# Four reorderings in a hybrid decoder step: early weight sums, gate read-outs, subtractions and state copies moved

## The chip, the cores and the metric

The kernel runs on one core of a Trainium2 chip. Its engines are TensorE (PE; its weight loads are listed apart as PEld), VectorE (DVE), ScalarE (ACT), GpSimd (POOL) and SyncE (SP), which here only issues DMAs. Time is measured on the device, from the start to the end of one execution, in microseconds.

## The reference, cut to what matters

One inference step of a two-layer decoder over 1048 tokens (16 meta tokens, 1024 of a prompt, 8 samples), in float32, model width 1024.

- Layer 0 projects the input, runs gated linear attention and a diagonal complex state-space model (S5) side by side, joins both and projects back (`w_out_0`).
- Layer 1 is a Griffin block: `y = (h * gelu(gate)) @ w_out`, where `h` is a gated linear recurrence over 1536 channels and `gate` a projection of the normalised input.
- Each layer ends in a gated feed-forward: `x + (gelu(conv(gate)) * val) @ w_down` with `gate, val = split(rmsnorm(x) @ w_up)` and `d_ff = 2816`.

```python
def rmsnorm(x, g):
    y = xf * lax.rsqrt(jnp.mean(xf * xf, axis=-1, keepdims=True) + EPS)
    return (y * g).astype(x.dtype)
...
xr, xi = xr + Ar * x0r - Ai * x0i, xi + Ar * x0i + Ai * x0r     # S5
...
y = (h * jax.nn.gelu(gate)) @ w_out                             # layer 1
...
return x + (jax.nn.gelu(gate) * val) @ w_down, new_buf          # feed-forward
```

## The kernel before

Every operand of a large matmul is split into a high part (cast to fp32r on ScalarE) and a low part (the rest, subtracted on VectorE), and each product is three matmuls (`mm3`): high by high, high by low, low by high. Lines 128, 129 and 130 are these three. Line 85 is the cast, line 45 the helper `tt` through which every elementwise operation of two tensors goes, on VectorE or, with the argument `P`, on GpSimd; line 48 is its form with a scalar. So rows are told apart by tile names. Line 147 is `colsum`, a product with a matrix of ones.

Weights come by `load_w`: a DMA on SP into `wraw`, a ring of three buffers, then the split into `whi` and `wlo`, rings of six. Products land in PSUM banks of two rings of four: `bank`, and `p` (tag `aux`). Each engine works through its own instructions in a fixed order, which the tile framework writes down before the run: it goes by the order in which the code is traced, by ready times that it estimates, and by priority (`tc.high_priority()`). A queue that waits holds back all that stands behind it on the same engine.

**S5.** The 32 groups go in four blocks (`b` = 0 to 3). `states(b)` forms the inputs in PSUM, moves them to `s5VR`, rotates them (`s5WC`, `s5WS`), scans them on VectorE into `s5ZB` and rotates them back: `ZA` and `VC` hold the products, and four subtractions or additions of 64 rows write the state, shifted by one, into `s5XP`. Line 466 multiplies `s5XP`, line 465 the input. `s5XR` and `s5SO` are the samples' step and the final states. `tables(b + 1)` builds `s5E`, which TensorE turns in line 366. Projections of the same layer lie between the blocks.

**First output projection.** Eight tiles `X`, three chunks each, are added to out of PSUM, stored to `xdn`, squared for the norm (`sq` on ScalarE, `acc` on GpSimd), and cut in halves for a seven-product scheme of block matrix multiplication (`Seven`): `B11`, `B21`, `B22` are plain halves, `T1` to `T4` sums of halves. `sums` forms these from tiles `t`.

**Layer 1.** Eight steps (two halves of the tokens by four groups of channels). A step projects (`xr`), applies the previous step's output projection (`out`), forms the gates, runs the recurrence (`rec`, scan in line 1540), and projects the gate branch: `gelu_branch` fills a bank per chunk of 262 tokens with 24 matmuls and reads it out into `rgg`. `joined` multiplies both. In the second half `before` begins the next feed-forward's statistics for finished tiles.

**The last step and the second feed-forward.** `out` ends the sums of `X`; `after` squares each chunk, and `sums_in` cuts it for `Seven`, in two parts; for the last two pairs the second part is kept in `rest` and traced after `out`. `ffn_up` makes 22 tiles `hidden(t)`, each of seven products: `B11`, `B21`, `T2`, `T3`, `T1`, `B22`, `T4`. Tiles 0 and 1 do their first two products ahead. The weights of four products are sums of blocks, formed by `sums` on GpSimd from tiles `wA` into `wS`. These pools lie where `X` was.

Of the kernel before, what the change touches and what calls it, by code (L numbers as in the profile page):

```python
# [9 lines left out]
F32 = mybir.dt.float32  # L10
# [29 lines left out]
def hybrid_step_kernel(ctx: ExitStack, tc: tile.TileContext, a: dict):  # L40
# [341 lines left out]
    def s5_states(bi, d, tabs):  # L382
# [54 lines left out]
        A1 = d["A1"]  # L437
        tt(XR[:, 1], XR[:, 0], A1[:, 0, sl].unsqueeze(1).unsqueeze(3).to_broadcast([128, 2, NI, 8]), MUL)
        tt(XR[:, 2, 0], XR[:, 0, 1], A1[:, 2, sl].unsqueeze(2).to_broadcast([128, NI, 8]), MUL)
        tt(XR[:, 2, 1], XR[:, 0, 0], A1[:, 1, sl].unsqueeze(2).to_broadcast([128, NI, 8]), MUL)  # L440
        tt(XR[:, 1], XR[:, 1], XR[:, 2], ADD)
        tt(SO[:, :, :, 0:8], XR[:, 1], VR[:, :, :, 0:8], ADD)
        tt(ZA, ZB, wc, MUL)
# [3 lines left out]
        P.memset(XP[:, :, 0:1], 0.0)  # L447
        nc.sync.dma_start(out=XP[:, :, 130:138], in_=a["s5xh"][:, g0:g0 + NG])
        for ri in range(2):
            for par in range(2):  # L450
                rows = slice(par * 64, par * 64 + 64)
                xo = XP[ri * 64:ri * 64 + 64].rearrange("p (i two) c -> p i two c", two=2)[:, :, par]
                tt(xo[:, :, 1:130], ZA[rows, ri, :, 0:129], VC[rows, ri, :, 0:129], ADD if ri else SUB)
            tt(SO[:, ri, :, 8], ZA[:, ri, :, 129], VC[:, ri, :, 129], ADD if ri else SUB)
        P.dma_start(out=a["o_s5"][:, :, sl], in_=SO)
# [537 lines left out]
    class Seven(Stats):  # L993
# [18 lines left out]
        def sums(self, j, x1, x2, pool):  # L1012

            g1, g2 = (CV[:, self.gain + m:self.gain + m + 1] for m in (j, j + 4))
            b12, t1, t2 = (pool.tile([128, HALF], F32, name="t7", bufs=3) for _ in range(3))

            def gained(o, x, g):
                A.activation(out=o, in_=x, func=ACTF.Copy, scale=g)

            gained(t1, x1[:, :HALF], g1)  # L1020
            gained(b12, x1[:, HALF:], g1)
            tt(t1, b12, t1, SUB, P)
            gained(t2, x2[:, HALF:], g2)
            tt(b12, t2, b12, SUB, P)
            tt(t2, t2, t1, SUB, P)
            split(*self.o["T2", j], t2)
            split(*self.o["T3", j], b12)
            split(*self.o["T1", j], t1)
            gained(t1, x2[:, :HALF], g2)
            tt(t1, t1, t2, SUB, P)  # L1030
            split(*self.o["T4", j], t1)
# [69 lines left out]

    def ffn_up(layer, nx, fw=None):

        es = ExitStack()
        at = {}

# [4 lines left out]
        if fw:  # L1111
            at.update(wA=fw, wS=fw)
            places("fa", "p1", "R")
            places("fb", "VL", "C", "u2", "u4", "FC")
        else:
            places("fa", "wA")
            places("fb", "VL", "u2")
            places("fc", "wS")
            places("fd", "C", "u4", "FC")
            places("fe", "p1", "R")  # L1120
        fp = at["FC"]

# [3 lines left out]

        FC = fp.tile([128, NFF, 2, 8], F32, name="FC")
        pre = fp.tile([128, NFF, 8], F32, name="pre")
        fcp = fp.tile([128, NFF, 2], F32, name="fcp")
        pt = fp.tile([128, NFF, 8], F32, name="pt")  # L1130

# [19 lines left out]
        def sums(t):  # L1151
# [14 lines left out]
            out.append(new_piece())  # L1166
            split(*out[-1], s4_)
            return out

        def hidden(t):  # L1170
# [35 lines left out]
            if ahead:  # L1206
                yield
                ws2, ws3, ws1, ws4 = sums(t)
                w22 = plain(t, 1, 1)
                if t == 0:  # L1210
                    caches()
# [32 lines left out]
        for g in first:  # L1244
            next(g)
        for g in chain(first, (hidden(t) for t in range(2, NFF))):
            next(g)
# [307 lines left out]
    def gelu_branch(half, G, ws):  # L1555
        h0 = half * HALF
        ggs = []
        for w in ws:
            gg = rq.tile([128, HALF], F32, name="rgg", bufs=3)
            for c0, n in HCH:  # L1560
                p = bank()
                mm3(p[:, :n], kslices(w), cols(HL[half], c0, n))
                tt(gg[:, c0:c0 + n], p[:, :n], RB[:, h0 + c0:h0 + c0 + n], MUL)
            ggs.append(gg)
# [20 lines left out]
    def after(m, c0, n):  # L1585

        x = X[m][:, c0:c0 + n]
        if m in (0, 1, 4, 5):
            if m == 0:
                nxt.acc[c0] = tp.tile([128, 352], F32, name="acc", bufs=3)  # L1590
            sumsq_step(nxt.acc[c0], x, n, m == 0)
            if m == 5:
                tot[c0] = ps.tile([128, 512], F32, name="p", tag="aux", bufs=4)[:, :n]
                colsum(tot[c0], nxt.acc.pop(c0)[:, :n], last=False)
        else:

            q = tp.tile([128, 352], F32, name="sq", bufs=2)
            A.square(out=q[:, :n], in_=x)
            colsum(tot[c0], q[:, :n], first=False, last=m == 7)
            if m == 7:  # L1600
                A.activation(out=RB[:, c0:c0 + n], in_=tot[c0], func=ACTF.Sqrt, bias=eps, scale=1.0 / 1024)
                nxt.late.append((0, c0, n))
# [79 lines left out]
    out(*steps_[-1], prev)  # L1682
    for g in rest:
        next(g)
    nc.sync.dma_start(out=a["o_rcp"], in_=rcp)
    nc.sync.dma_start(out=a["o_rcs"], in_=RC)
    nc.sync.dma_start(out=a["o_h"], in_=hout)
    rps.close()
    xps.close()
    nx = nxt  # L1690

    back = ffn_up(1, nx)
    bms.close()
# [115 lines left out]
```

## Time and profile before

| | |
|---|---|
| runs, device us | 2488.47 median of 3 (2487.82 to 2498.07) |
| profiled execution, device us | 2490.02 |
| span of its trace, first to last instruction | 2488.2 |
| mean granted TensorE clock | 0.978 |
| busy: PE, PEld | 95%, 93% |
| busy: DVE, ACT, POOL | 72%, 46%, 24% |
| DMA | 277 MB, mean 111 GB/s |

The stages in the trace, in us from its start: S5 and the projections of layer 0 up to 250, attention up to 476, the first output projection up to 536 and the first feed-forward up to 1240, layer 1 up to 1724, its last step and the start of the second feed-forward up to 1800, the rest of that to the end. Idle time is that of an engine just before an instruction; what ended it stands behind the arrow.

### The profile page before, as it was taken

Reading aid. Unit: us, or ns where it says so; the run is one execution under the profiler, and the core shown is the slowest. Engines: PE = TensorE matmul, PEld = TensorE weight load, DVE = VectorE, ACT = ScalarE, POOL = GpSimd, SP = SyncE. Lnnn points to the kernel's source line nnn. Section 1 sums busy time; section 2 is a strip of 40 time slices with the busy share of each in tenths; the row PEclk is TensorE's granted clock in tenths of the full one; section 3 lists DMA queues with packets and bytes.
Section 4 is the critical chain, followed back from the end, with each engine's and each line's share of the span. In section 5 each row is a group of like instructions: output and inputs, shape, how many; then the busy total and the mean of one; then the engine's idle time right before and its main releaser. Section 6 shows DMA issues by size and latency. Waiting matters only on the chain.

```text
span 2488.2 us, 45222 instructions
## 1 busy us (share of the span) xinstructions
PE 2372.1 (95%) x17443; PEld 2326.2 (93%) x17443; DVE 1802.1 (72%) x3183; ACT 1139.8 (46%) x2302; POOL 589.9 (24%) x607
## 2 busy tenths in 40 slices
PE   6879999989999999999999999999799999999998
PEld 6768988879999999999999999998799999999997
DVE  9885788688777777554688777777877777766445
ACT  5224564554444444321576666665544444453123
POOL 4331000283443332000220002210333333310003
PEclk9999999989999999999999999999899999999999
DMA  3422225633333332632133333323333333336221
GB/s 117 108 70 80 87 71 168 212 128 122 118 116 116 116 116 94 211 109 89 43 90 94 99 99 122 93 89 100 128 116 116 116 116 116 116 119 195 90 82 70
DMA packets 200831, 277.09 MB, mean 111 GB/s; under 512 B 34440, under 2 KB 114264, under 8 KB 200616
## 3 DMA queue, kind: packets, MB, share of 16 engines
q1 hardware_dynamic: 191016, 261.94, 33.1%
q0 software_dynamic: 2848, 9.81, 1.0%
q10 hardware_dynamic: 6752, 2.45, 0.4%
q8 instruction: 137, 2.24, 0.4%
q14 instruction: 78, 0.64, 0.1%
HBM read 216.69 MB, written 51.43 MB: 108 GB/s over the span
## 4 chain that ended last, share of the span: by engine, by line
PE 74%; DVE 8%; issue 5%; DMA 3%; ACT 2%; POOL 1%; SPq 0%; DVEq 0%; POOLq 0%; ACTq 0%
PE bank L128 18%; PE bank L129 18%; PE bank L130 18%; PE p L128 6%; PE p L129 6%; PE p L130 6%; DVE X L45 1%; DVE wlo L45 1%; DVE rh L1540 1%; DMA hr<-hdr 1%; PE p L779 1%; DMA hr<-xdn 1%; DVE rig L48 0%; DMA SS<-in_st 0%; POOL acc L45 0%
## 5 line engine op out<-in xcount | busy, mean ns | idle before, releaser
L85 ACT CAST whi<-wraw 128x512 fp32r<-128x512 f32 (+2 forms) x449 | 262.1, 590 | 450.5 <-PE bank L129 328.0
L45 DVE TENSOR_TENSOR wlo<-wraw,whi 128x512 fp32r<-128x512 f32 (+2 forms) x448 | 327.9, 738 | 127.6 <-ACT whi L85 112.6
L45 DVE TENSOR_TENSOR X<-X,bank 128x352 f32<-128x352 f32 (+4 forms) x388 | 187.1, 486 | 194.8 <-PE bank L130 192.8
L128 PE MATMUL bank<-ph,whi 128*128 128x352 f32 (+1 forms) x912 | 293.1, 322 | 2.0 <-DVE X L45 1.8
L129 PE MATMUL bank<-pl,whi 128*128 128x352 f32 (+1 forms) x912 | 294.0, 322 | 0.0
L130 PE MATMUL bank<-ph,wlo 128*128 128x352 f32 (+1 forms) x912 | 293.7, 322 | 0.0
L45 POOL TENSOR_TENSOR acc<-acc,sq 128x352 f32<-128x352 f32 (+3 forms) x97 | 106.7, 1105 | 556.4 <-ACT sq L143 555.2
L85 ACT CAST whi<-wS 128x512 fp32r<-128x512 f32 x176 | 109.0, 620 | 262.2 <-PE p L129 127.1
L45 DVE TENSOR_TENSOR wlo<-wS,whi 128x512 fp32r<-128x512 f32 x176 | 125.2, 712 | 122.3 <-ACT whi L85 120.6
L128 PE MATMUL bank<-b,whi 128*128 128x262 f32 x560 | 164.2, 293 | 18.3 <-DVE rgg L45 9.8
L128 PE MATMUL bank<-H,whi 128*128 128x352 f32 (+1 forms) x480 | 161.4, 339 | 18.0 <-DVE X L45 8.1
L128 PEld LDWEIGHTS bank<-ph,whi 128*128 128x128 f32 x912 | 171.3, 188 | 3.2 <-DVE X L45 2.6
L129 PEld LDWEIGHTS bank<-pl,whi 128*128 128x128 f32 x912 | 171.3, 188 | 0.8
L130 PEld LDWEIGHTS bank<-ph,wlo 128*128 128x128 f32 x912 | 171.3, 188 | 0.0
L45 POOL TENSOR_TENSOR wS<-wA 128x512 f32<-128x512 f32 x88 | 151.5, 1721 | 69.5 <-DVE wlo L45 60.7
L129 PE MATMUL bank<-L,whi 128*128 128x352 f32 (+1 forms) x480 | 160.9, 337 | 7.0 <-DVE L L48 7.0
L130 PE MATMUL bank<-b,wlo 128*128 128x262 f32 x560 | 163.0, 291 | 3.9 <-DVE wlo L45 3.9
L129 PE MATMUL bank<-b,whi 128*128 128x262 f32 x560 | 163.1, 291 | 0.0
L128 PE MATMUL bank<-a,whi 128*128 128x262 f32 x560 | 160.5, 287 | 0.4 <-DVE rgg L45 0.4
L130 PE MATMUL bank<-H,wlo 128*128 128x352 f32 (+1 forms) x480 | 158.9, 333 | 1.7 <-DVE wlo L45 1.7
L129 PE MATMUL bank<-a,whi 128*128 128x262 f32 x560 | 159.9, 285 | 0.0
L130 PE MATMUL bank<-a,wlo 128*128 128x262 f32 x560 | 159.2, 284 | 0.0
(474 smaller groups left out, 7982.6 us busy)
## 6 DMA issues: line engine op xcount, KB each, us to landing
wA<-in_w_up SPq DMA_DIRECT2D x176, 256.0 KB, 2.7
wraw<-in_w_up SPq DMA_DIRECT2D x132, 256.0 KB, 4.8
wraw<-in_w_in SPq DMA_DIRECT2D x96, 256.0 KB, 2.8
hr<-hdr SPq DMA_DIRECT2D x44, 524.0 KB, 3.9
hdr<-VL SPq DMA_DIRECT2D x42, 524.0 KB, 4.0
wraw<-in_w_dn SPq DMA_DIRECT2D x80, 256.0 KB, 2.9
wraw<-in_w_out SPq DMA_DIRECT2D x48, 256.0 KB, 2.6
hr<-xdn SPq DMA_DIRECT2D x16, 524.0 KB, 3.6
```

The costliest lines, as they stand in the source:

```text
L45: return (eng or V).tensor_tensor(out=o, in0=x, in1=y, op=op)
L85: A.copy(out=h, in_=x)
L128: PE.matmul(out=out, lhsT=wh, rhs=xh, start=first and i == 0, stop=False, **kw)
L129: PE.matmul(out=out, lhsT=wh, rhs=xl, start=False, stop=False, **kw)
L130: PE.matmul(out=out, lhsT=wl, rhs=xh, start=False, stop=last and i == n - 1, **kw)
L779: PE.matmul(out=pas[c // 2][j0:j0 + m, c % 2, hp, :, j0 // 2:j0 // 2 + x], lhsT=lv[:, hp, c * C + j0:c * C + j0 + m], rhs=qz[:, :, hp, c * ...
L1540: V.tensor_tensor_scan(out=r[:, :npr], data0=av[:, :npr], data1=ig[:, :npr], initial=hprev[:, t:t + 1], op0=MUL, op1=ADD)
```

## The change

It has five parts.

1. In `gelu_branch` the read-out of a bank gets high priority.
2. `ffn_up` of layer 1 forms the first tile's weight sums by `sums_early`, in place in three (then a fourth) buffers of the ring `wraw`, right after the first two products of tiles 0 and 1 and before `rest`; `rest` and the closing of the pool of `X` move into `between`. The tiles `p1` and `R` come from a pool on the other side. `small` makes the four small tiles later.
3. In `after` the partial sum `acc` enters the colsum last, in place of first.
4. In `Seven.sums` four subtractions per pair go from GpSimd to VectorE.
5. In `s5_states` five small operations go from VectorE to GpSimd; the state is combined in place in `ZB`, two operations of 128 rows, and brought to `XP` by four DMAs, two on SP and two on ScalarE's queue; one GpSimd copy takes the last column.

```diff
-        tt(XR[:, 1], XR[:, 0], A1[:, 0, sl].unsqueeze(1).unsqueeze(3).to_broadcast([128, 2, NI, 8]), MUL)
+        tt(XR[:, 1], XR[:, 0], A1[:, 0, sl].unsqueeze(1).unsqueeze(3).to_broadcast([128, 2, NI, 8]), MUL, P)
...
+        tt(SO[:, :, :, 0:8], XR[:, 1], VR[:, :, :, 0:8], ADD, P)
...
         for ri in range(2):
+            tt(ZB[:, ri], ZA[:, ri], VC[:, ri], ADD if ri else SUB)
             for par in range(2):
-                rows = slice(par * 64, par * 64 + 64)
                 xo = XP[ri * 64:ri * 64 + 64].rearrange("p (i two) c -> p i two c", two=2)[:, :, par]
-                tt(xo[:, :, 1:130], ZA[rows, ri, :, 0:129], VC[rows, ri, :, 0:129], ADD if ri else SUB)
-            tt(SO[:, ri, :, 8], ZA[:, ri, :, 129], VC[:, ri, :, 129], ADD if ri else SUB)
+                (nc.sync if par else A).dma_start(out=xo[:, :, 1:130], in_=ZB[par * 64:par * 64 + 64, ri, :, 0:129])
+        P.tensor_copy(out=SO[:, :, :, 8], in_=ZB[:, :, :, 129])
...
-            tt(t1, b12, t1, SUB, P)
+            tt(t1, b12, t1, SUB)
...
+        def sums_early(t):
+            r = {}
+            def get(i, k):
+                r[i, k] = wp.tile([128, 512], F32, name="wraw")
+                nc.sync.dma_start(out=r[i, k], in_=block(t, i, k))
+                return r[i, k]
+            a21, a22, a11 = get(1, 0), get(1, 1), get(0, 0)
+            tt(a22, a21, a22, ADD, P)
+            tt(a21, a11, a21, SUB, P)
+            tt(a11, a22, a11, SUB, P)
+            out = []
+            for x in (a11, a21, a22):
+                out.append(new_piece())
+                split(*out[-1], x)
+            a12 = get(0, 1)
+            tt(a12, a12, a11, SUB, P)
...
-                ws2, ws3, ws1, ws4 = sums(t)
+                ws2, ws3, ws1, ws4 = pre_sums.pop(t, None) or sums(t)
...
+        if not fw:
+            pre_sums[0] = sums_early(0)
+            between()
+            places("fa", "wA")
+            places("fb", "VL", "u2")
+            places("fc", "wS")
+            places("fd", "C", "u4", "FC")
+        FC, pre, fcp, pt = small()
...
-                tt(gg[:, c0:c0 + n], p[:, :n], RB[:, h0 + c0:h0 + c0 + n], MUL)
+                with tc.high_priority():
+                    tt(gg[:, c0:c0 + n], p[:, :n], RB[:, h0 + c0:h0 + c0 + n], MUL)
...
-            if m == 5:
+        else:
+
+            if m == 2:
                 tot[c0] = ps.tile([128, 512], F32, name="p", tag="aux", bufs=4)[:, :n]
-                colsum(tot[c0], nxt.acc.pop(c0)[:, :n], last=False)
...
-            colsum(tot[c0], q[:, :n], first=False, last=m == 7)
+            colsum(tot[c0], q[:, :n], first=m == 2, last=False)
             if m == 7:
+                colsum(tot[c0], nxt.acc.pop(c0)[:, :n], first=False)
...
-    for g in rest:
-        next(g)
...
-    xps.close()
+    fes, fe = open_pool("fe1", "right")
...
+    def between():
+        for g in rest:
+            next(g)
+        xps.close()
+    back = ffn_up(1, nx, None, fe, between)
```

## Rows read from the trace of the kernel before

**Rows 1.** Waits of TensorE, whole span: total us, times, longest.
```profile
PE p L366 <- DVE s5E L45: 15.4, 6, 4.6
PE bank L128 <- DVE X L45: 10.9, 10, 2.1
PE bank L128 <- DVE rgg L45: 10.2, 5, 3.5
PE bank L128 <- ACT whi L85: 8.5, 1, 8.5
PE p L147 <- POOL acc L45: 7.1, 2, 4.4
...
PE p L466 <- DVE s5XP L45: 5.0, 2, 4.7
```

**Rows 2.** Waits of TensorE from 1500 to 1700 us, second half of layer 1.
```profile
PE bank L128 <- DVE rgg L45: 9.4, 3, 3.5
```

**Rows 3.** VectorE's timeline before the first gap's read-out: start, us, instruction.
```profile
1530.62 1.28 DVE L1540 TENSOR_TENSOR_SCAN rh<-ra,hprev,rig 128x516 f32<-128x516 f32 x1
...
1533.05 0.42 DVE L45 TENSOR_TENSOR rgg<-bank,RB 128x262 f32<-128x262 f32 x1
```

**Rows 4.** Busy time and instructions by stretch: us, engines, granted clock, DMA share, GB/s.
```profile
1526.00:1530.00 4.00, 4.00 (x35) 4.00 (x35) 4.00 (x7) 3.92 (x9) 3.31 (x3) 1.00 0.00 1
1533.50:1537.00 3.50, 3.48 (x16) 3.48 (x17) 3.15 (x9) 3.14 (x6) 0.00 (x0) 0.53 0.25 75
...
1778.40:1783.20 4.80, 4.75 (x22) 4.75 (x23) 2.98 (x4) 1.41 (x3) 3.96 (x3) 0.53 0.21 61
1783.20:1800.00 16.80, 16.80 (x140) 16.80 (x139) 13.96 (x18) 9.20 (x16) 8.83 (x9) 1.00 0.46 156
```

**Rows 5.** TensorE's timeline at the start of the second feed-forward.
```profile
1773.57 0.58 PE L128 MATMUL bank<-b,whi 128*128 128x262 f32 x1 [8.51 <-ACT whi L85]
...
1778.45 0.59 PE L130 MATMUL bank<-b,wlo 128*128 128x262 f32 x1 [3.86 <-DVE wlo L45]
```

**Rows 6.** VectorE's groups, 1765 to 1778.45 us: busy us, mean ns, idle before.
```profile
L955 DVE RECIPROCAL RB<-RB 128x262 f32<-128x262 f32 x2 | 3.6, 1777 | 0.0
L45 DVE TENSOR_TENSOR b<-X,b 128x524 fp32r<-128x524 f32 x4 | 2.8, 693 | 0.0
...
L45 DVE TENSOR_TENSOR R<-R,RB 128x524 f32<-128x524 f32 x2 | 1.6, 832 | 0.0
```

**Rows 7.** Busy time of one pair of tiles in the first output projection.
```profile
508.08:524.54 16.46, 13.74 (x74) 12.91 (x73) 14.94 (x15) 10.46 (x20) 13.12 (x13) 0.90 0.46 164
```

**Rows 8.** VectorE's groups in that stretch.
```profile
L48 DVE SCALAR_TENSOR_TENSOR B<-X,CV,B 128x524 fp32r<-128x524 f32 x3 | 6.4, 2134 | 0.8 <-ACT B L89 0.8
L45 DVE TENSOR_TENSOR T<-t,T 128x524 fp32r<-128x524 f32 x4 | 4.7, 1188 | 0.0
L45 DVE TENSOR_TENSOR X<-X,bank 128x352 f32<-128x352 f32 (+1 forms) x6 | 3.0, 505 | 0.0
```

**Rows 9.** GpSimd's groups in that stretch.
```profile
L45 POOL TENSOR_TENSOR t<-t,t 128x524 f32<-128x524 f32 x5 | 6.9, 1389 | 1.5 <-ACT t L1018 1.4
L45 POOL TENSOR_TENSOR acc<-acc,sq 128x352 f32<-128x352 f32 (+1 forms) x6 | 6.6, 1102 | 0.6 <-ACT sq L143 0.5
```

**Rows 10.** VectorE's timeline at the end of `states(1)`.
```profile
152.41 1.42 DVE L45 TENSOR_TENSOR s5XP<-s5ZA,s5VR 64x516 f32<-64x516 f32 x2
...
154.54 5.20 DVE L45 TENSOR_TENSOR s5XR<-s5XR,s5A 128x64 f32<-128x64 f32 x1
```

**Rows 11.** GpSimd's timeline there.
```profile
154.97 2.23 POOL L45 TENSOR_TENSOR s5ZA<-s5WB,s5WK 128x520 f32<-128x520 f32 x2
```

**Rows 12.** The tile `s5XR`: its load's time on SP (ns), and to landing.
```profile
L436 SPq DMA_DIRECT2D s5XR<-in_s5xr x4: 607/610/692, 18.3 to 179.9; - x4
...
DMA to landing us min/median/max: 2.1/2.1/4.3
```

**Rows 13.** SP's timeline in the second block.
```profile
148.42 14.36 SPq L113 DMA_DIRECT2D wraw<-in_w0v  x2
```

More of the change, by code (lines that the diff above doesn't have):

```diff
@@ L437, in s5_states @@
         A1 = d["A1"]
-        tt(XR[:, 1], XR[:, 0], A1[:, 0, sl].unsqueeze(1).unsqueeze(3).to_broadcast([128, 2, NI, 8]), MUL)
[L439 to L442, printed above, removed]
+        tt(XR[:, 1], XR[:, 0], A1[:, 0, sl].unsqueeze(1).unsqueeze(3).to_broadcast([128, 2, NI, 8]), MUL, P)
+        tt(XR[:, 2, 0], XR[:, 0, 1], A1[:, 2, sl].unsqueeze(2).to_broadcast([128, NI, 8]), MUL, P)
+        tt(XR[:, 2, 1], XR[:, 0, 0], A1[:, 1, sl].unsqueeze(2).to_broadcast([128, NI, 8]), MUL, P)
+        tt(XR[:, 1], XR[:, 1], XR[:, 2], ADD, P)
+        tt(SO[:, :, :, 0:8], XR[:, 1], VR[:, :, :, 0:8], ADD, P)
         tt(ZA, ZB, wc, MUL)
@@ L1021, in sums @@
             gained(b12, x1[:, HALF:], g1)
-            tt(t1, b12, t1, SUB, P)
+            tt(t1, b12, t1, SUB)
             gained(t2, x2[:, HALF:], g2)
-            tt(b12, t2, b12, SUB, P)
-            tt(t2, t2, t1, SUB, P)
+            tt(b12, t2, b12, SUB)
+            tt(t2, t2, t1, SUB)
             split(*self.o["T2", j], t2)
@@ L1029, in sums @@
             gained(t1, x2[:, :HALF], g2)
-            tt(t1, t1, t2, SUB, P)
+            tt(t1, t1, t2, SUB)
             split(*self.o["T4", j], t1)
@@ L1100, in turned, with ffn_up @@
         return ph, pl
-    def ffn_up(layer, nx, fw=None):
+    def ffn_up(layer, nx, fw=None, fe=None, between=None):
         es = ExitStack()
-        at = {}
+        at, pre_sums = {}, {}
         def places(name, *tags):
@@ L1115, in ffn_up @@
         else:
[L1116 to L1121, printed above, removed]
+            at.update(p1=fe, R=fe)
         def cw(j, t):
@@ L1125, in cw, with small @@
             return CV[:, c:c + 1]
[L1127 to L1130, printed above, removed]
+        def small():
+            fp = at["FC"]
+            return (fp.tile([128, NFF, 2, 8], F32, name="FC"), fp.tile([128, NFF, 8], F32, name="pre"),
+                    fp.tile([128, NFF, 2], F32, name="fcp"), fp.tile([128, NFF, 8], F32, name="pt"))
         def caches():
@@ L1167, in sums @@
             split(*out[-1], s4_)
+            return out
+        def sums_early(t):
[14 more added lines that the diff above has]
+            tt(a12, a12, a11, SUB, P)
+            out.append(new_piece())
+            split(*out[-1], a12)
             return out
@@ L1591, in after @@
             sumsq_step(nxt.acc[c0], x, n, m == 0)
-            if m == 5:
+        else:
+            if m == 2:
                 tot[c0] = ps.tile([128, 512], F32, name="p", tag="aux", bufs=4)[:, :n]
-                colsum(tot[c0], nxt.acc.pop(c0)[:, :n], last=False)
-        else:
             q = tp.tile([128, 352], F32, name="sq", bufs=2)
             A.square(out=q[:, :n], in_=x)
-            colsum(tot[c0], q[:, :n], first=False, last=m == 7)
+            colsum(tot[c0], q[:, :n], first=m == 2, last=False)
             if m == 7:
+                colsum(tot[c0], nxt.acc.pop(c0)[:, :n], first=False)
                 A.activation(out=RB[:, c0:c0 + n], in_=tot[c0], func=ACTF.Sqrt, bias=eps, scale=1.0 / 1024)
@@ L1688, in hybrid_step_kernel @@
     rps.close()
-    xps.close()
+    fes, fe = open_pool("fe1", "right")
     nx = nxt
-    back = ffn_up(1, nx)
+    def between():
[3 more added lines that the diff above has]
+    back = ffn_up(1, nx, None, fe, between)
+    fes.close()
     bms.close()
```

## The prediction

> **What bounds the kernel now.** I read the busy shares first, then the waits of the matrix engine, then stretch by stretch what stands in front of each long wait. TensorE is busy for 95% of the span (the table above), so time can only come out of its idle stretches and of the slow matmuls behind them. The waits of TensorE [rows 1] put nearly all of its idle time at five places that this change touches. The S5 stage waits for VectorE's `s5E` (15.4 us) and `s5XP` (5.0 us). The first output projection waits for VectorE's additions to `X` (most of 10.9 us). The gate branch waits for `rgg` (10.2 us). The start of the second feed-forward waits for one cast of a weight sum (8.5 us) and then for its low part (3.9 us [rows 5]). Two sums of squares wait for GpSimd's `acc` (7.1 us).
>
> Each wait costs more than its idle time. Before a gap of the gate branch 35 matmuls take 4.0 us (0.114 each) at a granted clock of 1.00; after it 16 take 3.5 us (0.219 each) at 0.53, that is at the lower of the two levels, 1.2 GHz, for about that long [rows 4]. Such a gap therefore costs another 16 x 0.105 = 1.7 us.
>
> **Gate branch (`gelu_branch`, high priority).** The edit moves the read-out of a bank, one operation of 0.42 us, ahead of the recurrence on VectorE. In the first of three gaps VectorE still ran a scan of 1.28 us and other pieces of `rec` while TensorE's banks were full; the read-out came at 1533.05 [rows 3], and TensorE went on half a microsecond later. The three gaps hold 9.4 us [rows 2]; with 3 x 1.7 us of slow matmuls the edit can give at most 14.5 us. Nothing is added. What is late next is the recurrence, by 4 x 0.42 = 1.7 us; it feeds the output projection, which TensorE starts only after three tiles of the next projection, 3 x 2 x 24 matmuls of 0.114 = 16 us. That covers it; without the cover it would cost 1.7 us per step, 5 us in all. A read-out can still find a scan under way (1.28 us), so I count 12 us of the 14.5. Bounds: 0 and 14.5.
>
> **Early weight sums (`sums_early`, `between`) and the later sum of squares.** TensorE has nothing to do for 8.51 us, runs three matmuls, and stops for another 3.86 us [rows 5], first for the high part of a weight sum, then for its low part. In the new order the sums are traced ahead of `rest`, the last activation splits. They no longer wait for room in the region of `X`, and their casts no longer stand behind casts that wait for VectorE. But VectorE is busy through this whole stretch, so it remains the limit. From 1765 to 1778.45 it did, among others, two reciprocals (3.6 us), four `b` splits (2.8 us) and two products with `RB` (1.6 us) [rows 6]. The first product needs the last of the T2 tiles, one kind of `b`. I count for it the four `b` splits and as much again to form what they split, 5.6 us: TensorE starts near 1771. Its 24 matmuls then run at 0.219, 5.3 us, and end at 1776. Before, the product ended near 1783 (the last 22 took 4.8 us from 1778.4 [rows 4]). That is 7 us. The deferred reciprocals and products come back while VectorE is already busy for 14.0 of 16.8 us [rows 4], so I give 1 us back: 6 us. Bounds: 0, and 8.5 + 3.9 + 22 x 0.105 = 14.7 us.
>
> The three early operations on GpSimd (nearest row: 1.39 us for a subtraction of 524 columns [rows 9]) replace three that ran there anyway. The colsum of `acc` is put last, which removes its wait of 2.7 us out of the 7.1, but TensorE then reaches the gap above sooner and waits there: 0, at best 2.7 us. A further load waits in the weights' ring for one of three buffers; while SP waits, the loads of the next tile's sums stand behind it. They are not needed before TensorE has done four products of 24 matmuls, 4 x 24 x 0.114 = 11 us, which hides it; without that cover the cost is one transfer, some 3 us.
>
> **Subtractions of `Seven.sums` moved from GpSimd to VectorE.** One pair of tiles takes 16.46 us, in which VectorE is busy for 14.94 and GpSimd for 13.12 [rows 7]. The same operations take far longer on VectorE than alone: a `B` split 2134 ns and a `T` split 1188 ns [rows 8], where an undisturbed split of this size takes 693 ns [rows 6]. By that price 3 `B`, 4 `T` and 2 weight splits are 6.2 us, with 6 additions of 0.505 us 9.3 us [rows 8]. So 14.94 - 9.3 = 5.6 us are stretch, against 13.5 us of GpSimd arithmetic [rows 9]: 0.42 us per microsecond. Afterwards VectorE has four subtractions more, 12.1 us, and GpSimd only `acc`, 6.6 us, which stretches it by 2.8 us: 14.9 us, the same as now. I count 0. Without any stretch a pair would be bound by TensorE's 13.74 busy us [rows 7], 2.7 us less, or 11 us over four pairs.
>
> The Trainium skill's page SBUF — State Buffer, section SBUF: two separate sides, says that an operation of VectorE with two SBUF inputs and a GpSimd operation that reads SBUF exclude each other for the whole instruction. By that the edit would cost 3.8 us a pair (rival 3) in place of nothing. The trace agrees only in part, with 0.42, since GpSimd waits too and additions out of PSUM keep 0.505 us.
>
> **S5.** Per block VectorE does two combinations of 128 rows in place of four of 64 (two of them 1.42 us [rows 10]) and loses five small operations and two stores of the last column. One of the small ones took 5.20 us, while GpSimd was computing beside it [rows 10, 11]; that stall will fall on whatever VectorE does next, so I count about 0.2 us for each. VectorE gains some 1.4 + 1.2 = 2.6 us. Against it, the state now reaches `s5XP` by copies. Each queue issues two of 0.61 us, and a transfer of the nearest kind lands after 2.1 us [rows 12]: 3.3 us against 1.4 before the last of them is in, 1.9 us later. In the first two blocks `s5E` decides next, and it comes 2.6 us sooner: -5 us. In the third the copy decides: +2 us. The fourth is covered by matmuls. Sum -3 us; bounds -15 (all of the `s5E` wait) and +6 (three blocks at 1.9, none returned). GpSimd's five small operations are hidden, since it waits for VectorE in this stage; if not, they add about 5 x 0.2 us per block.
>
> **Sum.** 12 + 6 + 0 + 3 = 21 us off the profiled execution's own 2490.02 us (span 2488.2 us and 1.8 us around it): 2469.0. That execution was 1.55 us above the median of the runs, so against the median I expect 2467.5, rounded to 2468.
>
> **Rivals.**
>
> 1. The early sums do not help: VectorE has not formed the T2 tiles before the old time, since it was never idle there. For it: that full VectorE [rows 6]. Against it: 5.2 us of its work in the stretch is reciprocals and products with `RB`, which the first product does not need. Time: 6 us more, 2474.
>
> 2. The read-outs stay late, since the order on VectorE is written before the run and a stretched recurrence (a scan behind GpSimd's sums) can still lie ahead. Against it: four banks, each with 24 matmuls (2.7 us) of room. Time: 12 us more, 2480.
>
> 3. GpSimd's `acc` blocks VectorE for all its length: 12.1 + 6.6 = 18.7 us a pair in place of 14.9, 4 x 3.8 = 15 us more, 2483. Against it: 0.42 in the present stretch. This is the rule of the page named above.
>
> 4. Slower than before: the new copies queue behind a weight load on SP. SP stood from 148.42 to 162.78 at two loads [rows 13], while the state was ready at 153.8; a copy behind them would land at 162.8 + 0.6 + 2.1 = 165.5, 11.7 us late, in three blocks 35 us. Then 2467.5 + 35 makes 2503. It is decided by whether the copies are placed ahead of the load that waits. Against it: that load waits for a split which VectorE does behind the state, so the copy should be the first to be ready.
>
> 5. Nearly all waits go: 14 us at the gate branch, 12 at the feed-forward, 3 at the first projection, 6 in S5: 35 us, 2453.
>
> **How the numbers follow.** Chances: the forecast 0.54 (its own range 2460 to 2476), rivals one to five 0.14, 0.08, 0.08, 0.06 and 0.10. The range 2456 to 2486 leaves out the slow rival and the better half of the last, and holds 8 in 10. Half a percent, about what a measurement of this kernel can tell from no change, is 12.4 us: below 2476.0 lie nearly all of the forecast, most of rival one and all of rival five, 0.71; above 2500.9 most of rival four, 0.05; the rest, 0.24, between.
>
> **What would show it.** Gate branch: no wait of TensorE for `rgg` over 1 us in the second half, and clock 1.00 there. Feed-forward: one wait of some 6 us for a `b` split in place of 8.5 and 3.9 us for weights. First projection: `B` and `T` splits nearer to 0.7 us, but the stage as long as before. S5: waits for a DMA of `s5XP` of about 5 us, shorter ones for `s5E`. The prediction is wrong if TensorE still waits for `rgg`, if S5 grows by more than 6 us, or if VectorE's put-off work opens a new gap after 1790 us.

## The result and the profile after

The changed kernel took 2467.76 us (median of four runs, 2466.27 to 2473.13) against 2490.64 us (four runs, 2487.82 to 2498.07): a ratio of 0.9914, 95% interval 0.9899 to 0.9928. The forecast was 2468.0. The profiled execution took 2473.13 us, with a span of 2471.2 us; line 466 of before is L467 here.

The waits of TensorE after (total us, times, longest), against [rows 1]:

```profile
PE p L467 <- DMA s5XP<-s5ZB: 11.7, 2, 6.0
PE p L366 <- DVE s5E L45: 7.4, 4, 5.7
...
PE bank L147 <- POOL s5XP L447: 6.0, 1, 6.0
PE p L147 <- ACT sq L1626: 5.3, 3, 2.5
PE bank L128 <- ACT u L1212: 5.2, 2, 2.8
...
PE bank L128 <- DVE X L45: 4.6, 8, 0.9
...
PE bank L128 <- DVE rR L45: 3.6, 3, 1.6
```

The waits for `rgg` and for the weight sums are gone, those for `X` and `s5E` are halved. New are waits for the copied `s5XP`, for `sq`, for `u` and, small, for `rR`. What a stage gained can't be read off this list. So I cut both traces where TensorE starts the same matmul and took differences, here in us:

```
                       S5 and     projection,  rest of first  layer 1   last out,   rest
                       attention  first ffn up ffn, 1st step            second up
before                   475.88     515.16       256.22       477.13     496.35     267.52
after                    478.48     507.01       256.33       464.76     496.42     268.20
small S5 ops only        485.63     515.35       255.75       477.79     496.27     266.96
S5 copies only           478.04     514.96       254.81       476.89     497.36     267.02
subtractions only        475.46     507.05       254.05       475.61     496.43     266.97
gate priority only       475.81     515.39       256.83       464.64     497.64     267.04
early sums only          479.60     514.88       256.27       474.26     492.37     267.05
late square only         478.72     514.98       255.65       475.76     497.37     267.13
all but small S5 ops     475.13     507.11       254.80       464.71     496.25     266.99
the same, acc first      479.55     506.96       257.01       466.04     493.08     267.48
acc on VectorE           474.92     511.56       255.87       478.10     497.35     268.22
both on VectorE          477.75     509.04       254.58       477.98     496.29     267.83
rotation on VectorE      476.45     506.96       255.31       464.40     494.34     268.21
rotation, half of acc    475.51     505.77       254.96       465.03     495.56     267.11
```

One row is one profiled execution. Where the code of a column is the same, its values agree within 0.6 us in the projection, 1.3 in the last column, 3.0 in the third, 3.9 in layer 1, and 4.7 in the first (474.92 to 479.60 where S5 is as before). In the fifth column they agree within 1.4 us where it is as before, and within 2.1 (494.34 to 496.42) where it has both the early sums and the late square. Differences below that mean nothing. The projection gained 8.15 us, layer 1 gained 12.37 (11.8 between the means of the rows without the gate edit and of those with it), the second feed-forward nothing, and S5 nothing that can be told from its spread. The fences below show these four, all of the changed kernel unless another is named.

Layer 1 and one pair of the projection, by window (TensorE, weight loads, VectorE, ScalarE, GpSimd, granted clock, DMA):

```profile
1500.00:1700.00 200.00, 196.25 (x1592) 194.59 (x1592) 158.49 (x305) 139.59 (x253) 28.32 (x39) 1.00 0.32 98
513.64:528.15 14.51, 11.85 (x69) 10.55 (x67) 14.23 (x20) 10.35 (x20) 7.60 (x9) 1.00 0.46 170
```

VectorE's groups in that pair, against [rows 8]:

```profile
L48 DVE SCALAR_TENSOR_TENSOR B<-X,CV,B 128x524 fp32r<-128x524 f32 x3 | 3.5, 1175 | 0.1
L45 DVE TENSOR_TENSOR T<-t,T 128x524 fp32r<-128x524 f32 x4 | 3.0, 768 | 0.0
```

The start of the second feed-forward in TensorE's timeline, against [rows 5]:

```profile
1739.83 1.13 PE L147 MATMUL p<-sq,ones 128*128 128x262 f32 x2 [2.39 <-ACT sq L1626]
...
1762.42 0.39 PE L128 MATMUL bank<-T,whi 128*128 128x262 f32 x1 [2.84 <-ACT u L1212]
...
1784.36 0.59 PE L128 MATMUL bank<-B,whi 128*128 128x262 f32 x1 [2.36 <-ACT u L1212]
```

The same work by window, from the first matmul of the last `out` to that of the third tile, in the kernel before:

```profile
1724.38:1809.53 85.15, 69.35 (x501) 67.53 (x501) 73.63 (x113) 45.89 (x87) 33.56 (x40) 0.88 0.35 118
```

and after:

```profile
1706.58:1791.80 85.22, 73.70 (x501) 70.99 (x501) 73.30 (x113) 45.25 (x87) 35.48 (x40) 0.88 0.35 118
```

The same 501 matmuls, the same mean clock, the same length. TensorE idles 4.3 us less (15.8 to 11.5) and is busy 4.35 us longer: waits of 2.7, 8.5 and 3.9 us have become four of 2.4 to 2.8 and two below 0.7, and behind each of the four it works at a lower granted clock (0.72, 0.52, 0.66 and 0.53 in the 3.0 to 4.5 us that follow).

The four blocks of S5 in TensorE's timeline:

```profile
124.28 0.83 PE L467 MATMUL p<-s5XP,s5CA 128*128 128x138 f32 x2 [5.99 <-DMA s5XP<-s5ZB]
...
158.92 0.80 PE L467 MATMUL p<-s5XP,s5CA 128*128 128x138 f32 x2 [5.69 <-DMA s5XP<-s5ZB]
...
191.74 0.57 PE L467 MATMUL p<-s5XP,s5CA 128*128 128x138 f32 x1 [3.81 <-POOL s5SO L455]
...
222.98 0.47 PE L467 MATMUL p<-s5XP,s5CA 128*128 128x138 f32 x2 [3.36 <-DMA wraw<-in_w0f]
```

Waits of about 5 us for a DMA of `s5XP` were forecast; they came with 3.4 to 6.0 us, in the fourth block too, which had none before. The copies landed 2.6 to 5.7 us after their issue, 3.4 at the median. The releasers named in the last two are inferred; `s5SO` reads the same `ZB` as the copies.

### The profile page after: what moved, and what is told of

It is laid out like the page before. It is cut to its first block, busy times and chain, and to the rows that moved or that the text cites. A ratio compares the mean times of both kernels' runs of the same rounds, so it can differ in the third digit from the quotient of the medians.

```text
span 2471.2 us, 45242 instructions
## 1 busy us (share of the span) xinstructions
PE 2369.9 (96%) x17443; PEld 2324.2 (94%) x17443; DVE 1778.6 (72%) x3163; ACT 1137.4 (46%) x2302; POOL 576.7 (23%) x615
## 4 chain that ended last, share of the span: by engine, by line
PE 74%; DVE 11%; issue 6%; DMA 4%; ACT 3%; POOL 1%; SPq 0%; DVEq 0%; ACTq 0%; POOLq 0%
PE bank L128 18%; PE bank L129 18%; PE bank L130 18%; PE p L128 6%; PE p L129 5%; PE p L130 5%; DVE wlo L45 1%; DMA hr<-hdr 1%; DVE X L45 1%; DMA hr<-xdn 1%; PE p L780 1%; DVE L L48 1%; PE p L467 1%; DMA wraw<-in_w0f 0%; ACT whi L85 0%
## 5 line engine op out<-in xcount | busy, mean ns | idle before, releaser
L45 POOL TENSOR_TENSOR acc<-acc,sq 128x352 f32<-128x352 f32 (+3 forms) x97 | 97.6, 1009 | 580.8 <-ACT sq L143 579.8
L128 PE MATMUL bank<-b,whi 128*128 128x262 f32 x560 | 159.7, 285 | 0.0
L129 PE MATMUL bank<-b,whi 128*128 128x262 f32 x560 | 159.4, 285 | 0.0
```

What stands on the lines that cost most here:

```text
L45: return (eng or V).tensor_tensor(out=o, in0=x, in1=y, op=op)
L128: PE.matmul(out=out, lhsT=wh, rhs=xh, start=first and i == 0, stop=False, **kw)
L129: PE.matmul(out=out, lhsT=wh, rhs=xl, start=False, stop=False, **kw)
```

## The experiments

Medians of all runs with the ratio to the kernel before, timed on the same chip:

```
small S5 ops only        2499.26   1.0032 [1.0019, 1.0045]
S5 copies only           2490.65   1.0002 [0.9988, 1.0016]
subtractions only        2481.68   0.9965 [0.9949, 0.9981]
gate priority only       2481.31   0.9962 [0.9947, 0.9978]
early sums only          2486.06   0.9983 [0.9968, 0.9998]
late square only         2491.22   1.0004 [0.9991, 1.0017]
all but small S5 ops     2465.94   0.9903 [0.9881, 0.9925]
the same, acc first      2469.14   0.9913 [0.9893, 0.9932]
acc on VectorE           2487.15   0.9985 [0.9970, 1.0000]
both on VectorE          2484.62   0.9978 [0.9965, 0.9991]
rotation on VectorE      2463.28   0.9892 [0.9874, 0.9911]
rotation, half of acc    2468.79   0.9907 [0.9890, 0.9923]
```

### The two halves of the S5 edit

**Small operations only.**

```diff
...
-        tt(XR[:, 1], XR[:, 1], XR[:, 2], ADD)
+        tt(XR[:, 1], XR[:, 1], XR[:, 2], ADD, P)
...
```

> The kernel before, with only the five small operations of each S5 block moved from VectorE to GpSimd; the state still goes to s5XP by four VectorE operations of 64 rows. Theory (relief): in the trace of before one of the five took 5.20 us beside GpSimd's work, so VectorE comes to s5E sooner; TensorE's waits for s5E go from 15.4 us to about 8 (7.4 in the changed kernel), and the first matmul of the attention starts 3 to 6 us before its 232.0. Rival (the stall only moves): the next VectorE operation takes the stall over, s5E waits stay within 2 us of 15.4 and the attention starts within 1 us of 232.0. Whole time: 2484 to 2487 by the theory, 2489 to 2491 by the rival.

Both were wrong: the attention started at 239.73, 7.7 us later. The seven traces with the S5 code of before start it at 232.00 to 235.92, so this is the one variant outside the spread, and its whole time is longer by more than its interval. Waits for `s5E` grew from 15.4 to 17.9 us. VectorE's timeline of this run, here in the second block, shows that the stall was not taken along with the operation that had it:

```profile
158.47 0.68 DVE L45 TENSOR_TENSOR s5tm<-s5BB,s5Q 128x512 f32<-128x512 f32 x1
159.26 5.48 DVE L45 TENSOR_TENSOR s5E<-s5E,s5tm 128x512 f32<-128x512 f32 x1
164.66 2.08 DVE L45 TENSOR_TENSOR wlo<-wraw,whi 128x512 fp32r<-128x512 f32 x1
```

GpSimd's, at the same time:

```profile
159.49 2.23 POOL L45 TENSOR_TENSOR s5ZA<-s5WB,s5WK 128x520 f32<-128x520 f32 x2
161.60 1.35 POOL L45 TENSOR_TENSOR s5WC<-s5WC,s5ZA 128x520 f32<-128x520 f32 x1
162.83 1.34 POOL L45 TENSOR_TENSOR s5WS<-s5WS,s5ZA 128x520 f32<-128x520 f32 x1
164.05 1.02 POOL L339 MEMSET s5TT<- 128x1024 f32 x1
164.96 1.23 POOL L45 TENSOR_TENSOR s5CA<-s5CB,s5P 128x576 f32<-128x576 f32 x1
```

VectorE's operation, 0.68 us of work, lasts until GpSimd comes to its memset, and the next one lasts until `s5CA` is done. Before, `s5XR` stood in that place [rows 10, 11]; now `s5E` does, for which TensorE waits. In the first and third block the stall fell on weight splits (5.80 us for a `wlo`, 5.24 for a `whi`). A second loss is in GpSimd's queue, where `s5XR` got ahead of the statistics' `acc`:

```profile
35.92 0.33 POOL L45 TENSOR_TENSOR s5XR<-s5XR,s5A 128x64 f32<-128x64 f32 x1 [0.76 <-DVE s5A L290]
36.32 0.32 POOL L45 TENSOR_TENSOR s5XR<-s5XR 128x64 f32<-128x64 f32 x1
36.60 1.21 POOL L45 TENSOR_TENSOR acc<-acc,sq 128x352 f32<-128x352 f32 x1
```

TensorE's wait for that `acc` is 5.93 us in place of 3.79, as in the changed kernel (5.99).

**Copies only.**

```diff
-                tt(xo[:, :, 1:130], ZA[rows, ri, :, 0:129], VC[rows, ri, :, 0:129], ADD if ri else SUB)
...
+            tt(ZB[:, ri], ZA[:, ri], VC[:, ri], ADD if ri else SUB)
...
+                (nc.sync if par else A).dma_start(out=xo[:, :, 1:130], in_=ZB[par * 64:par * 64 + 64, ri, :, 0:129])
...
```

> The kernel before, with only the other half of the S5 edit: the state is combined in place in two operations of 128 rows and brought to s5XP by four DMAs; the five small operations stay on VectorE. Theory (copies cost): each block waits for a DMA of s5XP of 3 to 6 us, the fourth too, where no wait stood before; the small operations now stand ahead of the same combinations, so nothing comes back; the attention starts 4 to 8 us after 232.0, which is more than the 2.3 us of the whole S5 edit. Rival (the copies are neutral, the small operations on GpSimd are what costs): the attention starts within 1 us of 232.0 here. Whole time: 2495 to 2498 by the theory, 2490 by the rival.

The attention started at 231.74, just below the 232.00 to 235.92 of the S5 code of before: the theory fell, the rival held. The waits at `s5XP` grew from 4.69, 2.87 and 2.94 us to 8.34, 4.70 and 4.63, together by 7.2; the waits for `s5E` fell from 15.4 to 7.4, by 8.0. In the second block `s5E` starts 0.7 us after the state is combined (151.94 against 151.24); before, it started 5.8 us after that (159.67 against 153.83), behind the `s5XR` of 5.20 us [rows 10]. The longest operation there is now an `s5XR` of 2.57 us, and it stands behind `s5E`.

**All edits, the small operations back on VectorE.** Against the changed kernel:

```diff
...
-        tt(XR[:, 1], XR[:, 1], XR[:, 2], ADD, P)
+        tt(XR[:, 1], XR[:, 1], XR[:, 2], ADD)
...
```

> The changed kernel with the five small operations of each S5 block put back on VectorE; the copies and all other edits stay. Alone, the small operations on GpSimd took 7.7 us more up to the attention, and the copies alone took nothing. Theory (the two halves add, at least in part: the small operations ahead of acc in GpSimd's queue cost 2.2 us in the statistics, the rest later in s5E): the attention starts 2 to 3 us before the 234.3 of the changed kernel, with the wait behind the memset of s5XP back at 3.8 from 6.0 us and the copies' waits as they are; whole time 2464 to 2466. Rival (with the copies in place it makes no difference which engine does them): 2467.5 to 2468.

230.86 and 2465.94 us, with the wait in the statistics back at 3.76, as the theory had it. Only that wait is shown: the whole time's interval overlaps that of the changed kernel, and the last run of the section on the early sums below, whose S5 code is the same, starts the attention at 233.06 against the 234.26 of the changed kernel.

**The rotation on VectorE too.** Against the kernel just shown:

```diff
-        tt(w4(ZA[:, 0]), wb(1), wk(1), MUL, P)
-        tt(WC, WC, ZA[:, 0], SUB, P)
+        tt(w4(ZA[:, 0]), wb(1), wk(1), MUL)
+        tt(WC, WC, ZA[:, 0], SUB)
...
```

> The changed kernel with the small S5 operations back on VectorE, and with four of the six operations that form s5WC and s5WS moved from GpSimd to VectorE. In every trace so far the first VectorE operation with two SBUF operands behind the state takes 5.0 to 5.5 us (s5XR, wlo or s5E), as long as GpSimd runs these four back to back. Theory (the run of GpSimd is the stall): no VectorE operation over 2.5 us is left between 100 and 200 us; four operations of some 0.7 us stand in its place, so VectorE is 2 us a block sooner and the attention starts 2 to 6 us earlier than without the move (230.9 in that trace); whole time 2460 to 2464. Rival (VectorE is needed for the rotation just when it is the one waited for, so its 2.7 us more per block cost as much as the stall): the attention starts within 2 us of 230.9, whole time 2465 to 2467.

In the kernel that this one was made from, VectorE's timeline in the second block reads:

```profile
151.36 1.55 DVE L45 TENSOR_TENSOR s5E<-s5E,s5tm 128x512 f32<-128x512 f32 x1
152.83 2.67 DVE L45 TENSOR_TENSOR s5XR<-s5XR,s5A 128x32 f32<-128x32 f32 x2
...
157.25 0.68 DVE L45 TENSOR_TENSOR wlo<-wraw,whi 128x512 fp32r<-128x512 f32 x1
```

With the rotation on VectorE it reads:

```profile
151.03 1.30 DVE L45 TENSOR_TENSOR s5ZA<-s5WB,s5WK 128x520 f32<-128x520 f32 x2
152.25 0.69 DVE L45 TENSOR_TENSOR s5WC<-s5WC,s5ZA 128x520 f32<-128x520 f32 x1
152.86 0.69 DVE L45 TENSOR_TENSOR s5WS<-s5WS,s5ZA 128x520 f32<-128x520 f32 x1
153.47 0.41 DVE L45 TENSOR_TENSOR s5XR<-s5XR,s5A 128x64 f32<-128x64 f32 x3
153.81 0.68 DVE L45 TENSOR_TENSOR wlo<-wraw,whi 128x512 fp32r<-128x512 f32 x1
```

"In every trace so far" was wrong: with the copies in place the longest operations of VectorE before the attention are 3.05, 2.57 and 2.79 us, not 5.0 to 5.5. In this run none is over 2.5. From the first `s5XR` (151.18) to the end of the second `wlo` (157.93) VectorE took 6.75 us there; here the same operations and 2.7 us of rotation take 5.2 (150.00 to 155.23). So the theory's cause is shown: without GpSimd's run beside it VectorE is not held up. Its gain is not shown: the attention started at 231.17, as the rival had it, and at 234.12 in the last run of the next section, which has the same S5 code. TensorE still waits for the copies (4.96, 4.39, 4.51 and 3.58 us).

### Who does what in the first output projection

**Subtractions only.**

```diff
-            tt(t1, b12, t1, SUB, P)
+            tt(t1, b12, t1, SUB)
...
```

> The kernel before, with only the four subtractions of each pair in Seven.sums moved from GpSimd to VectorE. Theory (GpSimd's arithmetic stretches VectorE's by more than 0.42 us per us, and TensorE becomes the bound of the stage): a pair takes about 14.5 us in place of 16.46, T splits 0.8 us in place of 1.19, and B11 of the first feed-forward starts 7 to 9 us sooner relative to the first output projection (before: 476 to 537); whole time 2481 to 2483. Rival (what was predicted: the subtractions cost VectorE what the stretch gives back, so the stage keeps its length): within 1.5 us, 2489 to 2491. Second rival (the gain in the changed kernel's stage came from another part): also no change here.

The column is 8.1 us shorter, splits of `T` take 767 ns, a pair takes 14.53 us, and no other stage changed by more than its spread: the theory.

**`acc` on VectorE, subtractions on GpSimd.**

```diff
-            sumsq_step(self.acc[c0], x, n, m == 0)
+            sumsq_step(self.acc[c0], x, n, m == 0, eng=self.eng)
...
+    nx.eng = V
```

> The kernel before, where in the first output projection the additions to acc go from GpSimd to VectorE and the subtractions stay on GpSimd: the mirror image of the edit of Seven.sums. In the trace of before a B split of VectorE took 3.95 us while GpSimd ran four operations back to back (acc, t, acc, t). Theory one (what counts is how long GpSimd runs without a pause while VectorE wants two operands): GpSimd keeps only the subtractions, with waits for ScalarE between them, no split takes over 2.5 us, and a pair takes 14.5 to 15.3 us in place of 16.46; B11 of the first feed-forward 4 to 8 us sooner relative to the first output projection. Theory two (the subtractions themselves, slow on GpSimd, are the chain that the stage waits for): no gain, 16 us or more a pair, since VectorE takes 3 us more. Whole time 2483 to 2487 by the first, 2490 to 2492 by the second.

A pair took 14.5 to 15.4 us, by which of its three `B` splits one counts (503.13 to 517.61, 505.30 to 520.66), and no split took more than 1.8. `B11` came 4.1 us sooner, at the lower end of the first theory, but the column gained only 3.6: at the end TensorE waited 5.01 us for `acc`, which had been 4.41. This speaks for the first theory, with a smaller gain. In the kernel before, VectorE's longest `B` split

```profile
508.08 3.95 DVE L48 SCALAR_TENSOR_TENSOR B<-X,CV,B 128x524 fp32r<-128x524 f32 x1 [0.84 <-ACT B L89]
```

lay beside this of GpSimd:

```profile
507.99 1.32 POOL L45 TENSOR_TENSOR t<-t,t 128x524 f32<-128x524 f32 x1
509.27 0.94 POOL L45 TENSOR_TENSOR acc<-acc,sq 128x352 f32<-128x352 f32 x1
510.18 1.28 POOL L45 TENSOR_TENSOR t<-t,t 128x524 f32<-128x524 f32 x1
```

and ended 0.6 us after it.

**Both on VectorE,** the two diffs above together.

> The kernel before, where in the first output projection both the subtractions and the additions to acc go to VectorE; GpSimd does nothing there. By undisturbed prices VectorE then has about 15 us a pair. Theory one (mutual exclusion is the price, VectorE's sum the bound): splits at 0.7 us throughout, a pair 14.8 to 15.3 us, that is 1 to 2 us over four pairs worse than with the subtractions alone; whole time 2483 to 2486. Theory two (TensorE and the chain set the pair at 14.5): as with the subtractions alone, 2481 to 2482.

Splits took 0.7 us and the whole time was 2484.62, as theory one had it, but the pair is as neither had it. From one addition to `acc` on VectorE to the same one of the next pair it took 12.57 us, in which neither TensorE nor VectorE ever waits,

```profile
499.72:512.29 12.57, 12.57 (x81) 12.57 (x80) 12.57 (x25) 11.07 (x21) 1.06 (x2) 1.00 0.51 173
```

and TensorE did the 72 matmuls of a pair in 11.5 (502.18 to 513.65). But the column gained 6.1 us in place of 8.1: the sums of the last pair were late, and the first feed-forward waited 6.44 us for a `wlo` behind them.

**Half of `acc` on VectorE,** on top of the rotation.

```diff
+            sumsq_step(self.acc[c0], x, n, m == 0, eng=V if m % 4 < self.eng else P)
...
+    nx = Seven(0); nx.eng = 2
```

> The kernel of the run with the S5 rotation on VectorE, and in addition the acc additions of the first two of the four pairs in the first output projection on VectorE. With all of them on VectorE a pair took about 12.6 us in place of 14.5, but TensorE then waited 6.4 us for a weight split behind the last pair's sums. Theory (GpSimd's additions still cost VectorE its turns; the loss at the end came from the last pairs' work piling up): the first two pairs take 12.5 to 13.2 us each, TensorE's wait at the start of the first feed-forward stays at 2 to 4 us, and B11 of the first feed-forward starts 2 to 4 us sooner relative to the first output projection than in the run before (53.0 us there); whole time 2459 to 2462. Rival (VectorE's backlog is only carried over, whoever makes it): the first pairs are shorter, the last ones longer by as much, 52 to 54 us in all; whole time 2463 to 2465.

From the first output projection to B11 it took 49.3 us, 3.7 less, as the theory had it; 2.5 us of them were lost again before the end of the first feed-forward's first half, so 1.2 are left in the column, and the whole time, 2468.79, does not show them. It lies above the range of either side. So the stage up to `B11` bears out the theory and the whole time doesn't; that the rest of the 3.7 us is the backlog of the rival is not shown.

### The gate branch alone

```diff
+                with tc.high_priority():
+                    tt(gg[:, c0:c0 + n], p[:, :n], RB[:, h0 + c0:h0 + c0 + n], MUL)
```

> The kernel before, with only the high priority on the read-out of the gate branch's banks. Theory (the read-outs alone): no wait of TensorE for rgg over 1 us from 1500 to 1700 us, granted clock 1.00 there, the last out of layer 1 12 us sooner relative to the start of layer 1; whole time 2477 to 2480. Rival (the gain needs the later sum of squares or the shifted phase of the other edits): waits for rgg or for rR remain, half of the gain or less, 2483 to 2489.

Waits of TensorE from 1500 to 1700 us of this run:

```profile
PE bank L128 <- DVE rR L45: 3.6, 3, 1.7
```

There is no `rgg`, the clock is 1.00, and layer 1 is 12.5 us shorter: the theory, though the whole time, 2481.31, lies 1.3 us above its range. The `rR` waits, which the kernel before doesn't have, are what the put-off recurrence costs.

### Early sums and the order of squares

**Early sums only**: part 2 of the change on the kernel before. **Late square only**: part 3,

```diff
-                colsum(tot[c0], nxt.acc.pop(c0)[:, :n], last=False)
...
+                colsum(tot[c0], nxt.acc.pop(c0)[:, :n], first=False)
```

and then **all edits, the small S5 operations back on VectorE and part 3 undone**.

> The kernel before, with only the early weight sums (sums_early, between, the moved pools); acc still enters the sum of squares first. In the kernel with all edits the stretch from the last out to the third tile of the second feed-forward is as long as before (85.2 us against 85.15), although the waits of 8.5 and 3.9 us are gone. Theory one (the later sum of squares eats the gain: it turned one wait of 2.67 us into waits of 2.52, 0.42 and 2.39): without it the stretch is 4 to 6 us shorter, waits for u of 2 to 3 us may stay; whole time 2484 to 2487. Theory two (the put-off splits give the gain back: casts for T and the gelu stand ahead of the copies u on ScalarE): the stretch is within 1.5 us of 85.15 here too, with waits for u of 5 us together and lower granted clock behind them; whole time 2489 to 2491.

> The kernel before, with only the order of the sum of squares changed (acc enters last, the squares first). Theory one of the run on the early sums (this edit alone takes the gain): the wait of 2.67 us for acc becomes waits for sq of 4 to 6 us together, the 8.5 us wait for the weight sum shrinks by as much, since VectorE sets its end: whole time within 1.5 us of before, 2489 to 2492. Theory two: the same whole time, but the waits for sq stay near 2.7 us in sum or vanish. Rival from the prediction (at best the wait of acc goes): 2.7 us less.

> The changed kernel with the small S5 operations back on VectorE and with acc again first in the sum of squares. Theory one of the run on the early sums (the later sum of squares eats their gain): 4 to 5 us less than the run with the small operations back alone, 2460 to 2461, and the stretch from the last out to the third tile at 80 to 81 us. Theory two (the put-off splits eat it): within 1.5 us of that run, the stretch at 84 to 86 us.

The early sums alone take 492.37 and, with the other edits, 493.08 us from the last `out` to the second feed-forward's down projection, where 496.35 to 497.64 stood without them; with the late square as well it is 496.42, 496.25, 494.34 and 495.56. So the early sums give some 4 us and the late square takes about 3 of them (1.3 to 4.1, by which traces one compares), which is theory one. The late square alone costs nothing that shows (497.37): its wait for `sq` is 2.49 us in place of 2.67 for `acc`, as theory two of that run had it, and the wait for the weights behind it is still 8.4 us and ends 49.7 us after the start of the last `out` (before: 49.2). Of the 12.4 us of waits that the early sums remove, only 4 remain as gain: new waits for `u` come (timeline of the first of the three runs),

```profile
1778.10 0.59 PE L128 MATMUL bank<-T,whi 128*128 128x262 f32 x1 [4.56 <-ACT u L1211]
...
1800.23 0.39 PE L128 MATMUL bank<-B,whi 128*128 128x262 f32 x1 [2.35 <-ACT u L1211]
```

which is theory two's mechanism at a smaller price. The whole time of the third run (2469.14) was forecast at 2460 to 2461 and does not bear the 3 us out against 2465.94. The intervals overlap, and its trace lost 4.4 us in the first column, whose code is the same. So the 3 us are shown by the stage alone, in two traces on one side of the comparison and four on the other.

No version is shown to be faster than the changed kernel: 2463.28 has an interval, 0.9874 to 0.9911, that overlaps its own.

## Why the prediction was right, and where it wasn't

The total was right, in good part by luck: of its four terms one was right and two were wrong in opposite directions, and the fourth can't be told from the spread. In the profiled executions the stages sum to -17.05 us against -21; the medians lie 22.9 apart. One reading at its start was wrong as well: the waits that it names are 61 us in all, about half of the 116 us in which TensorE was not busy (2488.2 us of span less 2372.1 busy), and not nearly all.

- **Gate branch, -12: right.** Layer 1 is 12.4 us shorter, 12.5 with this edit alone, 11.8 by the means of all rows. The wait and the slow matmuls behind it went as [rows 2, 4] said, and the recurrence came late by small waits (3.6 us in all) that the 12 of 14.5 had room for.
- **Subtractions, 0: wrong by 8 us.** VectorE's sum was nearly right: 14.9 us a pair forecast, 14.23 measured. The step that failed was to take that sum for the length of the pair: before, a pair was 16.46 us with VectorE busy for 14.94 [rows 7], and its 1.5 us of idle time, 0.8 of it for ScalarE [rows 8], were counted as if they would stay. They fell to 0.3: 0.7 + 1.2 us a pair, four pairs, some 8 us. That the moved subtractions fill those places is read from the timelines, not shown by a run. TensorE's own bound, which I put at 13.74 us from a stretch at clock 0.90, was too high as well: with both on VectorE it did a pair's matmuls in 11.5 us at clock 1.00.
- **Rival three, the full block, fell.** A pair became 2 us shorter and not 3.8 longer. The Trainium skill's page SBUF — State Buffer, section SBUF: two separate sides, has the exclusion for a whole instruction. The trace agrees in that an operation of 0.68 us took 5.48, but that was over four instructions of GpSimd on end and not over one. My mean of 0.42 us per us of GpSimd hid that the price hangs on what stands beside what: in the pair after the change VectorE's 14.23 us are 2.1 above its 12.1, against 7.60 us of GpSimd, which is 0.28.
- **Early sums and the late square, -6: wrong, 0.** The mechanism of the first part was right (8.5 and 3.9 us went). Two terms were mis-sized. The give-back, put at 1 us, came as two waits for `u`, 5.2 us. For the first, ScalarE's copies stood behind casts that waited for GpSimd and VectorE,

```profile
1757.63 0.62 ACT L85 CAST whi<-wraw 128x512 fp32r<-128x512 f32 x1 [4.52 <-POOL wraw L45]
...
1761.46 0.63 ACT L85 CAST T<-X 128x524 fp32r<-128x524 f32 x1 [2.15 <-DVE X L45]
1761.99 0.65 ACT L1212 COPY u<-bank 128x262 f32<-128x262 f32 x2
```

  (the first is the cast of the fourth early sum, whose load I took to be hidden: it was, for TensorE's product, but not for ScalarE's queue; no run without it was made, so its share is not shown). And the late square, put at 0 or a gain, costs some 3 us as soon as no longer wait follows it. The forecast's wait of 6 us for a `b` split was 0.62. Its named failure, a new gap after 1790 us from put-off work, came: the last `out` starts 17.8 us sooner than before, so the gaps that end at 1762.42 and 1784.36 stand for 1780.2 and 1802.2 on the time of before. That put-off work makes the second of them is not shown. In effect it was rival one's price, without its reason.
- **S5, -3: not borne out.** With the copies alone, the waits at `s5XP` grew by 2.4 us a block where I had 1.9, and the waits for `s5E` fell by 8 where I had 5. The landing was mis-sized: 3.4 us at the median where I had 2.1, from the load of a smaller tile [rows 12]. The small operations, "hidden, since GpSimd waits for VectorE", are what failed: they stood ahead of `acc` in GpSimd's queue, 2.1 us in the statistics, and freed nothing that shows. "That stall will fall on whatever VectorE does next" was right where the small operations moved alone, and its price was left out: 5.80, 5.48 and 5.24 us, once on the `s5E` for which TensorE waits. Beside the copies most of the stall is gone: in the changed kernel VectorE's longest operation before the attention takes 3.13 us.
- **The copies behind a weight load** (rival four) did not happen: in the first two blocks SP issued them from 119.35 and 153.11 us on, while VectorE combined the state (118.17 to 120.84, 151.48 to 153.79).

## What to carry to other kernels

Before moving work between VectorE and GpSimd, read the two timelines side by side: count GpSimd's longest unbroken run beside VectorE operations with two SBUF operands, and count VectorE's idle slots, since moved work may fall into them for nothing (read from timelines here, not shown by a run). When a wait goes, list what stands behind it in the same queue and in the queues that feed it; an edit that cost nothing in the shadow of a longer wait has its price once that is gone. Cut traces at the same instruction of the busiest engine: a total that comes out as forecast says little about its terms.

## What the runs showed of the hardware

- A VectorE operation with two SBUF operands can be held up over several instructions of GpSimd in a row: 5.48 us for one of 0.68, across `s5ZA` twice, `s5WC` and `s5WS`; it ended beside a memset, which reads nothing. It is not always the whole row: with the copies in place and the small operations on VectorE, an `s5XR` took 2.57 us (from 152.83) beside `s5WC` and `s5ZA`, and the next `wlo` took 0.68 (from 155.43) although `s5WS` followed at 155.42, which itself took 1.83 us in place of 1.34. Additions out of PSUM in the first output projection kept 0.50 to 0.52 us in every trace.
- Fewer idle microseconds need not shorten a stage: 501 matmuls took 69.35 us busy with 15.8 us of idle time in few long pieces, and 73.70 with 11.5 in more and shorter ones.
- The S5 and attention stages, with the same code, took 474.9 to 479.6 us from one execution to the next. In two of these traces, the kernel before and the early sums alone, TensorE is idle for 46.4 and 46.1 us before the attention, but busy for 185.6 and 188.7, at a mean granted clock of 0.93 and 0.91. What makes the clock differ stays open.
